# A two-branch encoder block on one core: where its small preparations stand, and which engine does them

## The chip, the core and the metric

The kernel runs on one core of a Trainium2 chip. The engines that matter are TensorE (PE in the profile; PEld is its weight load), VectorE (DVE), ScalarE (ACT), GpSimd (POOL) and SyncE (SP), whose queue issues the transfers. Each engine takes its instructions strictly in the order in which they stand in its own queue, and waits at semaphores for the others. The metric is the time of one execution in microseconds of the device. Four threads of the text run through all stages: the 128 x 512 matmul in fp32r as the unit of TensorE's work, the order of each queue, the PSUM banks, and the SP queue.

## The reference

One layer over a sequence of 1024 tokens of width 1024, all in float32. `x` is normalised and modulated, projected once, run through two token mixers in parallel, merged by gates, and followed by a SwiGLU feed-forward part. Cut to what matters here:

```python
u = layer_norm(x) * (1.0 + sc1) + sh1
proj = u @ w_in            # q, f, i, g | z, xbc, dt | gate_a, gate_b
# HGRN2, 8 heads of 128 x 128 states: f = lb + (1 - lb) * sigmoid(f_logit)
S_t = diag(f_t) S_{t-1} + (1 - f_t) i_t^T ;  o_t = S_t^T q_t
y_a = rms_norm(o, w_gnorm) * silu(g) @ w_branch_a
# Mamba-2, 4 groups of 8 heads: xbc = silu(causal_dwconv(xbc))
S_t = exp(a_t) S_{t-1} + b_t (delta_t x_t)^T ;  y_t = S_t^T c_t + d x_t
y_b = rms_norm(y * silu(z)) * w_norm @ w_branch_b
h = (sigmoid(gate_a) * y_a + sigmoid(gate_b) * y_b) @ w_o
x = layer_norm(ALPHA * x + g1 * h)
u = layer_norm(x) * (1.0 + sc2) + sh2
x = layer_norm(ALPHA * x + g2 * (silu(u @ w_gate) * (u @ w_up)) @ w_down)
```

## The kernel before

**Matmuls.** Full float32 accuracy comes from three fp32r matmuls for each contraction tile: low by high, high by low, high by high (`Dense.mm`, L81 to L83). The high part of an operand is a cast on ScalarE, the low part a subtraction on VectorE or GpSimd (`split`, L190 to L192; for weights `Dense.load`, L75 and L76). Such an operand is late when either is late. A *unit* is 128 output columns: two halves of 512 tokens, each of eight contraction tiles. The three matmuls of one contraction tile are called a subunit below.

**Stages.** In the profiled execution they lie as follows. 0 to 127: layer norm, modulation and the front of the input projection. 127 to 355: the other blocks, taken in pairs by a scheme that saves matmuls (`rest`). 355 to 500: the projection of `i` with the Mamba step sizes. 507 to 827: HGRN. 827 to 1300: Mamba. From 1300: the two branches' output matmuls (`dqs`), the merged projection, the first residual norm (to 1715) and the feed-forward part.

**Front.** The tokens come as 512 and 512 (`th` 0 and 1). The first four pairs run on half 0 while half 1 is normalised. Then comes a loop over `k` of four (from L413): `modulate(1, k)` and `modulate(1, 4 + k)`, a difference `c` of two tiles (L418) and four derived operands t1 to t4 with their splits; behind each step one further pair in `early`, which forms its weight difference (`combo`), splits it, multiplies, copies the product to `p1s` on ScalarE (L403) and subtracts it from a tile `ge` on VectorE (L405). The loop runs until seven pairs are done. Half 0 of gate block 6 follows.

**Projection of i.** Three groups of 352 columns over eight chunks of tokens. Behind group 0 the whole of `step_sizes` stands in the order: a chain of small VectorE operations to `adt`, a product with a triangular matrix (L527), and two transposing batches (L538), each in the same single PSUM bank "m", which `mod_segment` uses too.

**HGRN.** Eight heads of eight chunks of 128 tokens. `score(h, ch)` makes a chunk's scores, one chunk ahead: matmuls of 64, 32 and 16 columns on arrays `e` and `eb`, a copy `sc` on ScalarE (L687), two masked copies on VectorE (L689), a transposition and its copy `ks` (L693). `output` multiplies the scores (`oT`, L709) and updates the state with `ks`. In between `Fill` puts subunits of the next head's f and q projection and of gate units, about four a chunk (`share`). `prep(h)` makes a head's cumulated logarithms: five activations of 128 x 1024, eight scans (L620), two subtractions of 128 x 1024 (L627, L628). `arrays(h, hf)` makes the operands of half a head in six steps: four of `e` (L649, L654), one of `eb` (L657, L660), one of `kd` and `qd`. At chunk 3 the whole `prep(h + 1)` stands in the order, and the steps of `arrays` follow by twos at chunks 0 to 2 (second half) and 4 to 6 (next head).

**Mamba.** Four groups of eight chunks; `prepare` transposes x (`trx`, L850) one chunk ahead, `mix` has the inter-chunk (`yx`) and intra-chunk (`yi`) products; twelve subunits a chunk fill in, among them the next group's x, B and C blocks. The convolution's taps are VectorE operations on each half; `held` keeps two finished blocks for one Silu of 128 x 1024 each, the last x block too (L137). `squares` multiplies half a group by `z` on GpSimd (L923), squares and sums; `finish` has two matmuls `smm`, the norm's factors and four stores `yb_d` on SP. For the last group `squares(3, 0)` stands behind chunk 5, and everything else behind chunk 7, with 8 subunits ahead of the last `smm` and 24 behind it.

The order in each queue follows from a scheduler that takes the code's order as its base.

## Time and profile before

| | us |
|---|---|
| median of 3 runs | 2356.25 (2351.94 to 2360.98) |
| the profiled execution's own time | 2355.2 |
| its span, first to last instruction | 2353.3 |
| TensorE busy in it | 2251.6 (96%), mean granted clock 0.980 |
| VectorE, ScalarE, GpSimd busy | 1573.2, 1036.3, 314.7 |

A row of the timeline has the start, the length, engine, line, operation and tiles; in brackets the idle time of the engine before it and who ended it. Matmuls overlap: a wide one of 0.39 us starts about every 0.23 us. A row of windows has the stretch and its length, then busy time with the number of instructions in brackets for PE, PEld, DVE, ACT and POOL, then the granted clock of TensorE (1.00 is full speed), the DMA share and GB/s. A row of waits has the total in microseconds, the number of times and the longest. A row of groups has the number of instructions, busy time, mean in ns, and idle time before them. A line number is that of the kernel before.

### The profile page before, as it was taken

What the parts mean: (1) busy time and instruction counts of PE and PEld (TensorE: products, weight loads), DVE (VectorE), ACT (ScalarE), POOL (GpSimd) and SP (SyncE); (2) the same over time, 40 slices, a digit from 0 to 9 for tenths busy, and PEclk for the clock granted to TensorE, in tenths of its full rate; (3) what the DMA queues carried; (4) which work ended last, traced back from release to release, by engine and by line L of the source; (5) the groups of instructions that cost most, each with busy time, mean ns of one, the idle gap of its engine ahead of it and who ended that gap; (6) DMA issues with size and microseconds to landing.
All of it is one profiled execution on the core that took longest, in us unless ns stands there. A gap on an engine that the chain in (4) does not pass through costs nothing.

```text
span 2353.3 us, 32121 instructions
## 1 busy us (share of the span) xinstructions
PE 2251.6 (96%) x12412; PEld 1827.9 (78%) x12412; DVE 1573.2 (67%) x2545; ACT 1036.3 (44%) x1832; POOL 314.7 (13%) x188
## 2 busy tenths in 40 slices
PE   7889999999999999998997999999999999999998
PEld 4678888877777787777775788888778888888886
DVE  5966655538878657888976434458887666653556
ACT  3533333037666645777776411123533333322221
POOL 0600010011212121322223000003410000000000
PEclk9999999999999999999999999999999999999999
DMA  7344325611111232334355744423132222244553
GB/s 277 100 141 140 126 91 176 228 39 51 55 55 60 77 99 72 116 124 123 130 158 169 232 155 140 139 94 139 72 131 99 94 72 91 79 146 146 175 190 132
DMA packets 119504, 290.22 MB, mean 123 GB/s; under 512 B 12084, under 2 KB 26932, under 8 KB 119352
## 3 DMA queue, kind: packets, MB, share of 16 engines
q1 hardware_dynamic: 119352, 288.19, 36.6%
q8 instruction: 97, 1.59, 0.3%
q14 instruction: 55, 0.45, 0.1%
HBM read 234.52 MB, written 53.62 MB: 122 GB/s over the span
## 4 chain that ended last, share of the span: by engine, by line
PE 73%; DVE 10%; ACT 6%; DMA 3%; POOL 1%; issue 1%; SPq 0%; DVEq 0%; POOLq 0%; ACTq 0%
PE dps L81 9%; PE dps L82 9%; PE dps L83 9%; PE fps L81 9%; PE fps L82 9%; PE fps L83 8%; PE dqs L82 4%; PE dqs L83 4%; PE dqs L81 4%; DVE eb L657 1%; PE hps L83 1%; PE hps L82 1%; PE hps L81 1%; PE yi L897 1%; DVE e L649 1%
## 5 line engine op out<-in xcount | busy, mean ns | idle before, releaser
L81 PE MATMUL dps<-uh,wl 128*128 128x512 f32 x800 | 332.7, 416 | 2.5 <-DVE ge L405 2.5
L83 PE MATMUL dps<-uh,wh 128*128 128x512 f32 x800 | 318.6, 398 | 0.0
L82 PE MATMUL dps<-ul,wh 128*128 128x512 f32 x800 | 318.0, 398 | 0.0
L76 POOL TENSOR_TENSOR wl<-raw,wh 128x1024 fp32r<-128x1024 f32 x50 | 130.5, 2609 | 551.6 <-ACT wh L75 464.9
L81 PEld LDWEIGHTS dps<-uh,wl 128*128 128x128 f32 x800 | 156.0, 195 | 37.4 <-issue 9.9
L83 PEld LDWEIGHTS dps<-uh,wh 128*128 128x128 f32 x800 | 153.2, 191 | 33.9
L82 PEld LDWEIGHTS dps<-ul,wh 128*128 128x128 f32 x800 | 153.8, 192 | 28.5 <-issue 0.9
L179 POOL TENSOR_TENSOR mv<-mv,kc 128x1 f32<-128x1 f32 x32 | 32.8, 1032 | 1024.2 <-DVE mv L178 1016.2
L82 PE MATMUL dqs<-yp,wh 128*128 128x512 f32 x384 | 149.4, 390 | 0.0
L81 PE MATMUL dqs<-yp,wl 128*128 128x512 f32 x384 | 148.4, 389 | 0.9 <-ACT yp L191 0.9
L83 PE MATMUL dqs<-yp,wh 128*128 128x512 f32 x384 | 149.1, 389 | 0.0
L191 ACT CAST cw<-raw 128x512 fp32r<-128x512 f32 x131 | 80.7, 621 | 130.0 <-PE fps L83 86.7
L81 PE MATMUL fps<-t,cw 128*128 128x512 f32 x352 | 137.0, 389 | 0.7 <-ACT p L1177 0.7
L82 PE MATMUL fps<-t,cw 128*128 128x512 f32 x352 | 136.9, 389 | 0.0
L83 PE MATMUL fps<-t,cw 128*128 128x512 f32 x352 | 136.9, 389 | 0.0
L75 ACT CAST wh<-raw 128x1024 fp32r<-128x1024 f32 x75 | 78.4, 1046 | 112.3 <-PE dqs L83 103.5
L82 PE MATMUL fps<-wl,hp 128*128 128x512 f32 x304 | 118.4, 389 | 0.0
L83 PE MATMUL fps<-wh,hp 128*128 128x512 f32 x304 | 118.3, 389 | 0.0
L81 PE MATMUL fps<-wh,hp 128*128 128x512 f32 x304 | 117.0, 390 | 0.5 <-ACT wh L191 0.5
L192 DVE TENSOR_TENSOR wl<-wdr,wh 128x1024 fp32r<-128x1024 f32 x38 | 46.5, 1224 | 105.0 <-ACT wh L191 105.0
L192 DVE TENSOR_TENSOR cw<-raw,cw 128x512 fp32r<-128x512 f32 x109 | 79.9, 734 | 41.6 <-ACT cw L191 40.3
L191 ACT CAST wh<-wdr 128x1024 fp32r<-128x1024 f32 x38 | 40.1, 1054 | 147.3 <-PE fps L83 146.1
(367 smaller groups left out, 5649.2 us busy)
## 6 DMA issues: line engine op xcount, KB each, us to landing
raw<-in_w_blk_dram SPq DMA_DIRECT2D x78, 512.0 KB, 3.3
wdr<-in_w_d_dram SPq DMA_DIRECT2D x44, 512.0 KB, 3.9
wa<-in_w_ada_dram SPq DMA_DIRECT2D x32, 512.0 KB, 4.5
ac<-ac_d SPq DMA_DIRECT2D x32, 512.0 KB, 5.0
raw<-in_w_g_dram SPq DMA_DIRECT2D x26, 512.0 KB, 3.9
raw<-in_w_u_dram SPq DMA_DIRECT2D x26, 512.0 KB, 3.4
hr<-h_d SPq DMA_DIRECT2D x44, 256.0 KB, 4.0
h_d<-sg SPq DMA_DIRECT2D x18, 512.0 KB, 2.9
```

The lines of the kernel that those rows point to most:

```text
L75: nc.scalar.copy(wh, raw)
L76: (eng or self.lo).tensor_tensor(wl, raw, wh.bitcast(F32), op=ALU.subtract)
L81: nc.tensor.matmul(ps, sl, mh, start=first, stop=False)
L82: nc.tensor.matmul(ps, sh, ml, start=False, stop=False)
L83: nc.tensor.matmul(ps, sh, mh, start=False, stop=last)
L179: G.tensor_tensor(mv[:, 2:3], mv[:, 1:2], kc[:, 2:3], op=ALU.pow)
L191: S.copy(hi, src)
L192: eng.tensor_tensor(lo, src, hi.bitcast(F32), op=ALU.subtract)
L649: V.tensor_tensor(d.rearrange("p (n h j) -> p n h j", h=2, j=c), view(e, t0, (2 * c, n), (T + c, 2), (1, c)), view(r, t0 // 4 + c // 4 - 1 ...
L657: V.tensor_tensor(d.rearrange("p h (n j) -> p h n j", j=8), view(e, t0, (T, 2), (8, TH // 8), (1, 8)), view(r, t0 // 4, (T // 4, 2), (2, T ...
L897: PE.matmul(yi[64 * e:64 * e + 64, j, :], xd[:, HP * hh:HP * hh + HP], ac[:, hh, :], start=True, stop=True)
```

## The change

It has six parts; from the branch stage on each queue has the same instructions in the same order.

1. Front: `early` splits on VectorE instead of GpSimd, as do `c` and t3 in the k loop; the affine modulation of half 1 goes to ScalarE; the two loads for each modulation step are issued one step earlier; half 0 of gate block 6, and of gate block 7 (formerly in HGRN's last chunks), stand inside the k loop at k = 1 and 3, with their weights' low part on VectorE.
2. `step_sizes` stops before its matmuls and goes on behind chunk 4 of group 1; the bank "m" becomes three.
3. HGRN: `prep(h + 1)` in five pieces at chunks 0 to 4, `arrays(h + 1, 0)` by threes at chunks 5 and 6; `finish` one chunk later; `ks` copied by ScalarE.
4. Gate block 7's first half is gone from HGRN's filler: 8 subunits fewer.
5. Mamba: the last x block of a group gets its Silu by halves, the first as soon as its convolution is done; `bt` copied by ScalarE.
6. Last group: `squares(3, 0)` behind chunk 4, `finish(3, 0)` behind chunk 6, the multiplications by `z` of the last half on VectorE, and 18 instead of 8 subunits ahead of the last `smm` in the code.

```diff
-        ps = psum.tile([P, TH], F32, tag="m", name="mps", bufs=1)
+        ps = psum.tile([P, TH], F32, tag="m", name="mps", bufs=3)
...
+        def load_mod(j):
+            for h in range(2):
+                nc.sync.dma_start(out=was[:, (2 * j + h) % 4], in_=w_mod[j, :, 4 * h:4 * h + 4, :])
...
         def modulate(th, kt):
             u = xT[th][:, kt, :]
-            V.tensor_scalar(u, u, modc[:, 8 + kt:9 + kt], modc[:, kt:kt + 1], op0=ALU.mult, op1=ALU.add)
+            if th:
+                S.activation(u, u, AF.Identity, bias=modc[:, kt:kt + 1], scale=modc[:, 8 + kt:9 + kt])
+            else:
+                V.tensor_scalar(u, u, modc[:, 8 + kt:9 + kt], modc[:, kt:kt + 1], op0=ALU.mult, op1=ALU.add)
...
             if j + 2 < KT:
                 modulation(j + 2)
+            if j + 3 < KT:
+                load_mod(j + 3)
...
-        def early(q, a11, a12, eng=G):
+        def early(q, a11, a12, eng=V):
...
-            G.tensor_tensor(c, u1, u0, op=ALU.subtract)
-            split(t3[0][:, k, :], t3[1][:, k, :], c, G)
+            V.tensor_tensor(c, u1, u0, op=ALU.subtract)
+            split(t3[0][:, k, :], t3[1][:, k, :], c, V)
...
+            if k % 2:
+                n = 6 + k // 2
+                for _ in dn.unit(dn.load(w_blk[B_GA + n]), uh, ul, gate_evac(0, n), (0,)):
+                    pass
...
-        for _ in dn.unit(dn.load(w_blk[B_GA + 6], eng=G), uh, ul, gate_evac(0, 6), (0,)):
-            pass
...
         V.scalar_tensor_tensor(a, delta, -1.0, hr[:, None, 1, :].broadcast_to([P, TT, 32]), op0=ALU.mult, op1=ALU.mult)
-        ps = pp.tile([P, TH], F32, tag="m", name="dtps", bufs=1)
+        yield
+        ps = pp.tile([P, TH], F32, tag="m", name="dtps", bufs=3)
...
+                if g == 1 and tt == 4:
+                    steps.drain()
             if g == 0:
-                step_sizes(sp, pp)
+                steps = Fill(step_sizes(sp, pp))
+                steps.to(1)
...
                 act(ef, ef, AF.Exp, scale=-1.0)
+                yield
                 act(b, ef, AF.Ln, bias=lb[:, 3, h:h + 1], scale=lb[:, 1, h:h + 1])
+                yield
                 for c in range(TT):
                     V.tensor_tensor_scan(b3[:, c, :], ones, b3[:, c, :], 0.0, op0=ALU.mult, op1=ALU.add)
+                    if c == TT // 2 - 1:
+                        act(ef, ef, AF.Ln, bias=lb[:, 4, h:h + 1], scale=lb[:, 5, h:h + 1])
+                        yield
                 act(eq, eq, AF.Ln, bias=kc[:, 4:5], scale=QS)
-                act(ef, ef, AF.Ln, bias=lb[:, 4, h:h + 1], scale=lb[:, 5, h:h + 1])
...
+                V.scalar_tensor_tensor(ef, ef, -110.0, b, op0=ALU.max, op1=ALU.subtract)
+                yield
                 V.tensor_tensor(eq, b, eq, op=ALU.subtract)
-                V.scalar_tensor_tensor(ef, ef, -110.0, b, op0=ALU.max, op1=ALU.subtract)
...
-                    V.tensor_copy(ks, sp_[:, 3, :])
+                    S.copy(ks, sp_[:, 3, :])
...
-                if ch == 3 and h + 1 < HA:
-                    prep(h + 1)
-                    nxt = arrays(h + 1, 0)
-                if ch % 4 < 3 if ch < 4 else (ch < 7 and h + 1 < HA):
-                    next(nxt, None)
-                    next(nxt, None)
-                if ch % 4 == 0 and i:
-                    finish(*((h, 0) if ch else (h - 1, 1)))
+                    ahead = chain(prep(h + 1), arrays(h + 1, 0)) if h + 1 < HA else iter(())
+                for gen, n in ((nxt, "22200000"[ch]), (ahead, "11111330"[ch])):
+                    for _ in range(int(n)):
+                        next(gen, None)
+                if ch % 4 == 1 and i > 1:
+                    finish(*((h, 0) if ch > 4 else (h - 1, 1)))
...
-                        if th and len(held) == 2:
+                        if th and len(held) == 2 or held[-1][0] == 4 * g + 3:
                             for k, t in held:
+                                if k == 4 * g + 3:
+                                    t = t[:, TH * th:TH * th + TH]
                                 act(t, t, AF.Silu, bias=cl[:, C_CB + k:C_CB + k + 1])
-                            held.clear()
+                            held[:] = held[1:] if len(held) == 2 and not th else []
...
-                    V.tensor_copy(bt, cb[:, 1, :])
+                    S.copy(bt, cb[:, 1, :])
...
-                    G.tensor_tensor(xT[:, j, sl], xT[:, j, sl], zs, op=ALU.mult)
+                    (V if g == GB - 1 and hf else G).tensor_tensor(xT[:, j, sl], xT[:, j, sl], zs, op=ALU.mult)
...
-                if g == GB - 1 and ch == 5:
+                if g == GB - 1 and ch == 4:
                     squares(g, 0)
+                if g == GB - 1 and ch == 6:
+                    finish(g, 0)
                 fill.to(share(i + 1))
-            finish(g, 0)
             squares(g, 1)
-            fill.to(total + 8)
+            fill.to(total + 18)
             finish(g, 1)
```

In the queues this stands as follows; a row has the line, the operation, the tiles and their shape, and xN for N like it in a row. Line numbers of the changed kernel are its own, up to 22 higher.

GpSimd's queue before, through the k loop of the front (`cw` are weight differences of `early`, `ge` is `c`, `t_643` is t3):

```order
L192 TENSOR_TENSOR cw<-raw,cw 128x512 x2
L179 TENSOR_TENSOR mv<-mv,kc 128x1
L192 TENSOR_TENSOR cw<-raw,cw 128x512 x2
L418 TENSOR_TENSOR ge<-xT_106 128x512
L192 TENSOR_TENSOR t_643<-ge,t_643 128x512
L192 TENSOR_TENSOR cw<-raw,cw 128x512 x2
L418 TENSOR_TENSOR ge<-xT_106 128x512
L192 TENSOR_TENSOR t_643<-ge,t_643 128x512
L192 TENSOR_TENSOR cw<-raw,cw 128x512 x3
L418 TENSOR_TENSOR ge<-xT_106 128x512
```

And in the changed kernel, from the same place on, behind the scalar work of the norms:

```order
L179 TENSOR_TENSOR mv<-mv,kc 128x1 x8
L76 TENSOR_TENSOR wl<-raw,wh 128x1024 x6
L760 TENSOR_TENSOR y<-y,sq 128x512
L76 TENSOR_TENSOR wl<-raw,wh 128x1024
L760 TENSOR_TENSOR y<-y,sq 128x512
L76 TENSOR_TENSOR wl<-raw,wh 128x1024
```

All splits of the front have left this queue; the next rows are low parts of weights (L76) and the HGRN outputs' multiplications.

VectorE's queue before, around the preparation of an HGRN head (`b`, `r` and `ab` belong to `prep`; `e`, `eb` and `qd` to `arrays`; `sc` is the masked copy and `S` the state of the head that runs):

```order
L192 TENSOR_TENSOR csl<-sq,csh 128x512
L620 SCALAR_TENSOR_TENSOR b<-mk,b 128x128 x8
L717 SCALAR_TENSOR_TENSOR S<-S,ebl,st_ps 128x128
L625 COPY r<-b 128x256
L626 TENSOR_SCALAR r<-b 128x256
L627 TENSOR_TENSOR ab<-b,ab 128x1024
L628 SCALAR_TENSOR_TENSOR ab<-ab,b 128x1024
L689 COPY_PREDICATED sc<-mk,sc_ps_3616 128x128
L649 TENSOR_TENSOR e_5474<-ab,r 128x512
L689 COPY_PREDICATED sc<-mk,sc_ps_3616 128x128
L693 COPY ks<-sc_ps_3616 128x128
L649 TENSOR_TENSOR e_5478<-ab,r 128x512
```

And in the changed kernel:

```order
L638 SCALAR_TENSOR_TENSOR b<-mk,b 128x128 x8
L682 TENSOR_TENSOR eb<-eb,xq 128x512
L711 COPY_PREDICATED sc<-mk,sc_ps_3654 128x128 x2
L739 SCALAR_TENSOR_TENSOR S<-S,ebl,st_ps 128x128
L645 COPY r<-b 128x256
L690 TENSOR_TENSOR qd<-qd,xq 128x512
L646 TENSOR_SCALAR r<-b 128x256
L647 SCALAR_TENSOR_TENSOR ab<-ab,b 128x1024
L711 COPY_PREDICATED sc<-mk,sc_ps_3653 128x128 x2
L739 SCALAR_TENSOR_TENSOR S<-S,ebl,st_ps 128x128
L649 TENSOR_TENSOR ab<-b,ab 128x1024
L671 TENSOR_TENSOR e_5114<-ab,r 128x512
```

Between the scans and the last subtraction of the preparation there now stand two chunks' masked copies and state updates, where there was one state update.

VectorE's queue before, from the last chunk of Mamba to the branch (`yt` combines the two products, L942 is the norm's multiplication, L927 the sum of squares, `csl` the split of the sums):

```order
L901 TENSOR_TENSOR yt<-yx,eb 128x512
L910 TENSOR_TENSOR yt<-yt,yi 128x512
L913 TENSOR_TENSOR xTm<-xTm,yt 128x4x128
L942 SCALAR_TENSOR_TENSOR xTm<-xTm,cl,sqs 128x512 x4
L927 TENSOR_TENSOR sqs<-sqs,zs 128x512 x3
L192 TENSOR_TENSOR csl<-sqs,csh 128x512
L942 SCALAR_TENSOR_TENSOR xTm<-xTm,cl,sqs 128x512 x4
L76 TENSOR_TENSOR wl<-raw,wh 128x1024
```

And in the changed kernel:

```order
L922 TENSOR_TENSOR yt<-yx,eb 128x512
L963 SCALAR_TENSOR_TENSOR xTm<-xTm,cl,sqs 128x512 x4
L931 TENSOR_TENSOR yt<-yt,yi 128x512
L934 TENSOR_TENSOR xTm<-xTm,yt 128x4x128
L944 TENSOR_TENSOR xTm<-xTm,zs 128x512 x2
L948 TENSOR_TENSOR sqs<-sqs,zs 128x512
L944 TENSOR_TENSOR xTm<-xTm,zs 128x512
L948 TENSOR_TENSOR sqs<-sqs,zs 128x512
L944 TENSOR_TENSOR xTm<-xTm,zs 128x512
L948 TENSOR_TENSOR sqs<-sqs,zs 128x512
L192 TENSOR_TENSOR csl<-sqs,csh 128x512
L76 TENSOR_TENSOR wl<-raw,wh 128x1024
```

The first half's multiplication by its norm (x4) moved ahead of the last chunk's combination, the multiplications by `z` (L944) came in from GpSimd, and a weight's low part stands ahead of the last norm's multiplications.

More of the change, by code (lines that the diff above doesn't have):

```diff
@@ L229, in mod_segment @@
                 if nh:
-                    ps = psum.tile([P, TH], F32, tag="m", name="mps", bufs=1)
+                    ps = psum.tile([P, TH], F32, tag="m", name="mps", bufs=3)
                 PE.matmul(ps[0:1, :], ones[:, 0:1], acc[:, TH * nh:TH * nh + TH], start=True, stop=True)
@@ L252, in gate_evac, with gate_units @@
         return evac
-    def gate_units(which, n0, n1, fine=False):
+    def gate_units(which, n0, n1, fine=False, ths=(0, 1)):
         for n in range(n0, n1):
-            yield from dn.unit(w_blk[(B_GA, B_GB)[which] + n], uh, ul, gate_evac(which, n, fine), fine=fine)
+            yield from dn.unit(w_blk[(B_GA, B_GB)[which] + n], uh, ul, gate_evac(which, n, fine), ths, fine=fine)
     def combo(pool, tag, src, eng=V, **k):
@@ L342, in hybrid_block @@
         V.tensor_copy(cond32[:, :, 0], cond)
+        for j in range(2):
+            load_mod(j)
         for tt in range(4):
-            if tt < 2 and MF > tt:
+            if tt < 2:
                 modulation(tt)
@@ L362, in hybrid_block @@
         for n in range(2):
-            if MF <= n:
-                modulation(n)
+            if n:
+                load_mod(2)
             for q in (2 * n, 2 * n + 1):
@@ L535, in step_sizes @@
         for hf in range(2):
-            ps = pp.tile([P, TH], F32, tag="m", name="dtps", bufs=1)
+            ps = pp.tile([P, TH], F32, tag="m", name="dtps", bufs=3)
             for j in range(4):
@@ L741, in hgrn_phase @@
             units = [dense_fq(h) for h in range(HA)]
-            fill = Fill(chain(*units, gate_units(0, 7, 8, True), gate_units(1, 0, NGB, True)))
+            fill = Fill(chain(*units, gate_units(0, 7, 8, True, (1,)), gate_units(1, 0, NGB, True)))
             fill.to(HF0)
-            prep(0)
-            for _ in arrays(0, 0):
-                pass
+            for g in (prep(0), arrays(0, 0)):
+                for _ in g:
+                    pass
             fill.to(HF1)
             score(0, 0)
-            total = 16 * (2 * HA + 1 + NGB)
+            total = 16 * (2 * HA + NGB) + 8
             def share(i):
@@ L756, in share @@
                 return a + (total - a) * (i - 8 * HA + 12) / 12
-            nxt = None
             for i in range(8 * HA):
```

5 lines of the change are left out of this document (3 added, 2 removed).

## The prediction

> **What bounds the kernel now.** I read the page's busy table first, then the waits of TensorE (PE), then windows of single stages.
>
> ```profile
> PE 2251.6 (96%) x12412; PEld 1827.9 (78%) x12412; DVE 1573.2 (67%) x2545; ACT 1036.3 (44%) x1832; POOL 314.7 (13%) x188
> 177.00:236.00 59.00, 59.00 (x262) 48.83 (x262) 40.68 (x64) 22.02 (x35) 0.00 (x0) 1.00 0.42 141
> 59.00:118.00 59.00, 48.84 (x195) 37.60 (x194) 53.79 (x65) 33.05 (x58) 40.53 (x25) 0.91 0.31 102
> ```
>
> TensorE is busy 96% of the span and sets the end. In a stretch without loss (second row) it issues 262 wide matmuls in 59.00 us, 0.225 us each. I call three of them, one contraction tile, a subunit: 0.68 us. Since the change leaves the number of matmuls as it is, it can gain only where TensorE waits, or runs at a lower granted clock behind a wait. In the front (last row) it issued 195, at a granted clock of 0.91 (the last but two of the columns), so (262 - 195) x 0.225 = 15 us were lost there. The waits name the other places:
>
> ```profile
> PE trx L850 <- ACT xTm L137: 13.5, 3, 6.7
> PE smm L936 <- DVE csl L192: 12.5, 1, 12.5
> PE dps L81 <- DVE cw L192: 10.2, 5, 4.9
> PE sc_ps L683 <- DVE eb L660: 7.6, 6, 1.4
> PE dps L81 <- DVE ge L405: 6.6, 3, 3.9
> PE dtps L527 <- DVE adt L524: 2.9, 1, 2.9
> ```
>
> The columns are microseconds in total, number of waits, longest. Each lies in a stage that the diff touches, except part of the third. They sum to 53 us.
>
> **Front: forecast -6 us.** The change takes all `early` splits and the t3 work from GpSimd to VectorE.
>
> ```profile
> L192 POOL TENSOR_TENSOR cw<-raw,cw 128x512 fp32r<-128x512 f32 x14 | 22.1, 1584 | 9.3 <-ACT cw L191 9.3
> L418 POOL TENSOR_TENSOR ge<-xT 128x512 f32<-128x512 f32 x4 | 9.0, 2251 | 2.9 <-DVE xT L318 2.9
> L192 POOL TENSOR_TENSOR t<-ge,t 128x512 fp32r<-128x512 f32 x4 | 6.0, 1504 | 3.7 <-ACT t L191 3.7
> 82.04 0.68 DVE L421 TENSOR_TENSOR xT<-xT,ul 128x512 f32<-128x512 f32 x1
> 82.64 0.67 DVE L405 TENSOR_TENSOR ge<-p1s,dps 128x512 f32<-128x512 f32 x1
> ...
> 88.40 1.77 DVE L421 TENSOR_TENSOR xT<-xT,ul 128x512 f32<-128x512 f32 x1
> ```
>
> The first three rows are GpSimd's groups in 59 to 118: 22 operations that VectorE now has to do. Then the same VectorE instruction without and with a GpSimd split running: 0.68 and 1.77 us; alone, the next one starts 0.60 behind it. So VectorE's 53.79 us of 59 hold 65 operations that alone would take 65 x 0.60 to 0.68, 39 to 44 us. After the change it has 22 more, and 4 to 8 fewer (the second half's modulate goes to ScalarE; eight in all, not all of them in this stretch): 79 to 83 operations, 47 to 56 us. TensorE's own work there is 195 x 0.225 = 44, and the gate half-unit moved in adds 24 x 0.225 = 5.4, with a split of a 128x1024 weight on VectorE (two such operations, 1.2 to 1.4), a cast, a load and a sigmoid. So the stretch, the half-unit inside, takes 49 on TensorE and 48 to 57 on VectorE, where it took 59: between -11 and -2. Waits of one for the other in order add to the larger of the two. I take -6, bounds -1 and -12. The modulation loads leave SP one step earlier; what they stand ahead of there are weight loads that are issued many steps before their use, so I cost them at nothing.
>
> The activation tables change four more times here. The row of a load (below, at 1200.26) is 1.28, and ScalarE was busy 33.05 of 59, so 5.1 us more hide in its idle time. Were that cover gone, all 5.1 would be added. The Trainium skill, "ScalarE: Activation LUTs", What ACT_TABLE_LOAD costs, adds a drain of about 1380 ns to each switch; the row behind the load below starts 1.29 after it, so the trace does not show it. By the page, and with nothing hidden, the sum would be 10.6 us higher.
>
> **Step sizes: -4 us.** The generator stops before its matmuls until chunk 4 of the next column group, and its tiles get three banks instead of one.
>
> ```profile
> 411.60 0.70 PE L527 MATMUL dtps<-adt,mk 128*128 128x256 f32 x2 [2.95 <-DVE adt L524]
> 415.24 1.63 PE L538 MATMUL dtps<-mk,adt 128*32 128x128 f32 x8
> ```
>
> The wait of 2.95 goes, since VectorE finishes `adt` long before chunk 4, and the lower clock behind a wait with it. With one bank, besides, the second batch of L538 must wait for the first's copy, which it need no longer. I put these two at 1 us together. Bounds -2 and -6.
>
> **HGRN heads: -22 us.** Each head costs the same 32 subunits before and after.
>
> ```profile
> 646.66 0.39 PE L709 MATMUL oT<-sc,i_sb 128*128 128x128 f32 x2
> ...
> 650.99 0.39 PE L709 MATMUL oT<-sc,i_sb 128*128 128x128 f32 x2
> ...
> 643.00:659.70 16.70, 16.70 (x194) 13.11 (x193) 10.20 (x26) 12.68 (x23) 3.85 (x2) 1.00 0.08 30
> 673.50:681.00 7.50, 6.12 (x63) 4.73 (x62) 7.47 (x11) 5.43 (x13) 2.04 (x1) 1.00 0.22 78
> 643.00:681.00 38.00, 36.43 (x392) 28.15 (x391) 31.48 (x68) 25.85 (x49) 8.22 (x4) 1.00 0.16 56
> 672.07 4.56 DVE L657 TENSOR_TENSOR eb<-ab,r 128x1024 f32<-128x1024 f32 x2
> 677.28 0.27 PE L683 MATMUL sc_ps<-eb 128*32 128x32 f32 x8 [1.38 <-DVE eb L660]
> L693 DVE COPY ks<-sc_ps 128x128 f32<-128x128 f32 x7 | 2.0, 283 | 0.0
> ```
>
> A chunk with four subunits takes 4.33 us (first two rows), so eight take 34.6, against 38.0 for a head: 3.4 lost, 27 over eight heads. The windows say where. In the first half of a head TensorE never rests and VectorE works 10.20 of 16.70; then a preparation arrives whole, and VectorE works 7.47 of 7.50 while TensorE waits for `eb`. The change spreads the preparation over chunks 0 to 4 and the arrays over 5 and 6, and gives the seven `ks` copies (2.0 us) to ScalarE. VectorE's demand falls to 29.5 of 34.6 us (85%), ScalarE's rises to 25.85 + 7 x 0.28 = 27.8 (80%): both fit, though engines that work in order at 85% still make TensorE wait at times. I leave 1.3 us a head, so 27 becomes 10: -17, and the gate half-unit that moved to the front is 5.4 us less here: -22. The bounds: the moved work and a little, -8; all stalls but 0.7 us a head, -27. `finish` moves one chunk later; its output is first read by the branch, which starts at 1315 (below).
>
> **Mamba edges: -5 us.**
>
> ```profile
> 1189.80 0.49 PE L850 MATMUL trx<-mk,xTm 128*128 128x128 f32 x3
> ...
> 1200.29 0.47 PE L850 MATMUL trx<-mk,xTm 128*128 128x128 f32 x1 [4.32 <-ACT xTm L137]
> ...
> 1191.56 0.63 ACT L925 ACTIVATE zs<-xTm 128x512 f32<-128x512 f32 x1 [2.34 <-POOL xTm L923]
> ...
> 1199.10 1.15 ACT L137 ACTIVATE xTm<-xTm,cl 128x1024 f32<-128x1024 f32 x1
> 1200.26 1.28 ACT L135 ACT_TABLE_LOAD   x1
> 1201.55 1.06 ACT L137 ACTIVATE ac<-ac 128x1024 f32<-128x1024 f32 x1
> ...
> 1190.12 0.74 DVE L813 SCALAR_TENSOR_TENSOR xTm<-dps,cl,xTm 128x509 f32<-128x509 f32 x1
> ```
>
> The first chunk of the next group needs only the first half of the last x block, but the Silu takes both, so the fourth transposition waits until 1200.25. The first half's convolution ends at 1190.86; a Silu of that half could end near 1192.8, behind the square at 1191.56. But the order now puts all four transpositions first, at 1189.80, so TensorE would meet a wait of some 3 us there in place of the 4.32. Over three edges the 13.5 becomes about 9 to 10, and the halved clock behind each costs as before: -5, bounds 0 and -12. The `bt` copies go the way of `ks` and are hidden by six subunits.
>
> **End of Mamba: -9 us.**
>
> ```profile
> 1272.69 1.54 PE L897 MATMUL yi<-ac,xd 128*64 128x128 f32 x16 [2.25 <-ACT csh L191]
> 1296.07 0.80 PE L936 MATMUL smm<-csl,ones_r 128*128 128x512 f32 x1 [12.49 <-DVE csl L192]
> 1284.27 2.50 SPq L943 DMA_DIRECT2D yb_d<-xTm  x4
> 1287.65 0.56 SPq L922 DMA_DIRECT2D zs<-z_d  x1
> 1291.99 1.26 POOL L923 TENSOR_TENSOR xTm<-xTm,zs 128x512 f32<-128x512 f32 x1 [8.29 <-DMA zs<-z_d]
> 1301.97 0.90 SPq L1008 DMA_DIRECT2D yr<-ya_d  x2
> L191 ACT CAST yp<-yr x8: 1033/1046/1052, 1307.1 to 1329.2; 128x1024 fp32r<-128x1024 f32 x8
> L81 PE MATMUL dqs<-yp,wl x21: 388/389/499, 1315.0 to 1329.4; 128*128 128x512 f32 x21
> ```
>
> From the last intra-chunk product (ends 1274.2) to the branch's first matmul (1315.0) are 40.8 us, with 3 + 8 + 24 = 35 subunits in TensorE's queue, 23.9 us. So 17 are lost: 12.49 waiting, the rest at the lower clock. The wait is for the fourth gating load `zs`, which stands on SP behind four stores of the first half, which wait for that half's norm. The change ends the first half in chunk 6, multiplies on VectorE (0.68 against 1.26) and puts 21 subunits (14.3 us) ahead of the sums. Without the 8.29 the chain of 21.9 us from 1274.2 to 1296.07 shrinks to about 13.5: hidden. But 14 subunits (9.5 us) remain behind the sums. There the old rows show what is late next: the loads `yr` leave SP only after the second half's stores, the first operand cast ends 12 us behind the sums (1308.1 - 1296.1), its VectorE split follows, and all eight take 22 more. I put a new wait there at 4 to 9 us, so of 17 I keep 9; bounds -2 and -14.
>
> **Sum.** -6 - 4 - 22 - 5 - 9 = -46 against the profiled execution's 2355.2 us: 2309. The median of the runs shown is 1 us above it, so 2310. From the branch stage on no instruction changes its order.
>
> **Rivals.** (1) HGRN stays bound by VectorE: it keeps 85% of the time, in order, and scans or `ab` operations between two chunks delay the masks just as `eb` did. Then the stage gains only the bound of 8, 14 less: 2324. For it: `sc_ps` already waits for `eb` in six places; against: the 16.70 of 16.70 beside a VectorE at 61%. (2) The branch's operands bind: the end of Mamba gains 2, not 9: 2317. For it speaks the row of 22 us; against, that 24 subunits hid nearly all of it and the stores now start earlier. (3) Slower: the `ks` copy stands on ScalarE behind long activations of the same preparation, and the state product needs it in each of 56 chunks. A 128x1024 activation takes 1.15 (the row at 1199.10). If every chunk lost that, 64 us would go: 2310 + 64 = 2374. It turns the forecast's sign above 46 / 56 = 0.82 us a chunk. Against it: the product stands two subunits (1.4 us) behind the scores, and a preparation has five such activations for eight chunks. (4) The table rule above, unhidden: 2310 + 10.6 = 2321.
>
> **How the numbers follow.** Forecast 0.60, rival 1 0.18, rival 2 0.11, rival 3 0.05, rival 4 0.01, the remaining 0.05 for several losses at once (about 2340). The likeliest case's own range: 2295 to 2322. For 8 in 10 the range runs from nearly all good bounds (2356 - 71 = 2285, taken as 2288) to rival 1 with the weak end of Mamba and little in the front (2356 - 22 = 2334). A measurement of this kernel tells 0.5%, 12 us, from no change. Rivals 1, 2 and 4 are still faster than that; rival 3 is no change between 0.6 and 1.0 us a chunk and slower above. Faster 0.90, same 0.06, slower 0.04.
>
> **What would show it.** After the change GpSimd has no 128x512 operation before 130 us, and VectorE's all take 0.7 or less there. The `dtps` wait is gone. `oT` starts every 4.3 us in all heads; a head of 37 or more with VectorE full proves rival 1. The `smm` wait is under 2 us, and a wait of `dqs` for `yp` names rival 2. A wait of `st_ps` for ScalarE's `ks` names rival 3. I am wrong if the time is above 2334, or if the stages from the branch on change their length by over 3 us.

## The result

The changed kernel takes 2317.6 us (median of four runs, 2310.2 to 2321.1) against 2355.0 for the kernel before beside it (four runs, 2351.9 to 2361.0): a ratio of 0.9834, interval 0.9803 to 0.9865. Run again on another occasion with more rounds it took 2318.9 against 2355.2, ratio 0.9845 (0.983 to 0.986). So it is faster by 1.6%, some 37 us. The forecast was 2310, 46 us less, with a range of 2288 to 2334.

The profiled execution of the changed kernel was the quickest of its four, 2310.2 us with a span of 2308.4, and 7 us below the median. One trace is therefore not enough to share 37 us out among stages. Twelve further traces of experiments (below) leave most stages as the changed kernel has them, and the mean over all traces whose code in a stage is that of the changed kernel is steadier. From the first matmul on, in microseconds:

| stage, from the order of TensorE | before | changed: mean (lowest to highest), traces | difference | forecast |
|---|---|---|---|---|
| front and pairs, to the i projection | 354.9 | 351.0 (349.8 to 351.6), 12 | -3.9 | -6 |
| i projection | 112.3 | 106.2 (103.2 to 107.6), 8 | -6.1 | -4 |
| HGRN, to its last `oT` | 345.6 | 324.1 (321.1 to 325.4), 11 | -21.5 | -22 |
| Mamba, first `trx` to group 3's first `yi` | 312.5 | 307.8 (305.8 to 312.4), 12 | -4.7 | -5 |
| group 3's first `yi` to the branch's last matmul | 365.3 | 366.0 (363.6 to 367.9), 9 | +0.7 | -9 |

They sum to -35.5, near the 37 of the medians. The column before has one trace.

### The profile page after: what moved, and what is told of

Same layout as the page of the kernel before. It is cut to its first block, busy times and chain, and to the rows that moved or that the text cites. A ratio compares the mean times of both kernels' runs of the same rounds, so it can differ in the third digit from the quotient of the medians.

```text
span 2308.4 us, 32125 instructions
## 1 busy us (share of the span) xinstructions
PE 2230.2 (97%) x12412; PEld 1816.2 (79%) x12412; DVE 1567.8 (68%) x2489; ACT 1061.6 (46%) x1931; POOL 264.8 (11%) x153
## 4 chain that ended last, share of the span: by engine, by line
PE 82%; DVE 8%; ACT 3%; issue 3%; DMA 2%; POOL 2%; SPq 0%; DVEq 0%; POOLq 0%; ACTq 0%
PE dps L81 11%; PE dps L83 11%; PE dps L82 11%; PE fps L81 9%; PE fps L82 9%; PE fps L83 9%; PE dqs L81 4%; PE dqs L83 4%; PE dqs L82 4%; PE hps L83 1%; PE hps L81 1%; PE hps L82 1%; PE sc_ps L701 1%; DVE xTm L832 1%; PE yi L918 1%
## 5 line engine op out<-in xcount | busy, mean ns | idle before, releaser
L81 PE MATMUL dps<-uh,wl 128*128 128x512 f32 x800 | 331.7, 415 | 3.3 <-POOL wl L76 3.3
L76 POOL TENSOR_TENSOR wl<-raw,wh 128x1024 fp32r<-128x1024 f32 x49 | 132.1, 2696 | 790.4 <-ACT wh L75 723.4
L81 PEld LDWEIGHTS dps<-uh,wl 128*128 128x128 f32 x800 | 155.1, 194 | 37.6 <-issue 6.6
L81 PE MATMUL dqs<-yp,wl 128*128 128x512 f32 x384 | 147.5, 393 | 6.6 <-ACT yp L191 4.3
L83 PE MATMUL dqs<-yp,wh 128*128 128x512 f32 x384 | 150.1, 391 | 0.0
L81 PE MATMUL fps<-t,cw 128*128 128x512 f32 x352 | 137.0, 389 | 0.7 <-DVE cw L192 0.7
L192 DVE TENSOR_TENSOR cw<-raw,cw 128x512 fp32r<-128x512 f32 x131 | 94.8, 725 | 43.5 <-ACT cw L191 42.2
L81 PE MATMUL fps<-wh,hp 128*128 128x512 f32 x304 | 117.0, 390 | 0.5 <-ACT wh L191 0.5
```

The source lines that it names most:

```text
L76: (eng or self.lo).tensor_tensor(wl, raw, wh.bitcast(F32), op=ALU.subtract)
L81: nc.tensor.matmul(ps, sl, mh, start=first, stop=False)
L83: nc.tensor.matmul(ps, sh, mh, start=False, stop=last)
L192: eng.tensor_tensor(lo, src, hi.bitcast(F32), op=ALU.subtract)
```

## The profile after

The busy line of the page and the longest waits of TensorE in the changed kernel (total, number of times, longest):

```profile
PE 2230.2 (97%) x12412; PEld 1816.2 (79%) x12412; DVE 1567.8 (68%) x2489; ACT 1061.6 (46%) x1931; POOL 264.8 (11%) x153
```

```profile
PE dps L81 <- DVE cw L192: 15.4, 9, 4.5
...
PE trx L871 <- ACT xTm L137: 7.4, 2, 4.0
PE dqs L81 <- ACT yp L191: 4.3, 1, 4.3
...
PE yi L918 <- ACT csh L191: 3.2, 1, 3.2
PE yx L910 <- DVE Sm L927: 3.0, 2, 2.5
...
PE dtps L539 <- issue: 2.1, 1, 2.1
```

The line of 12.5 us, `smm` for `csl`, is gone, and so are the six waits for `eb` and the three for `ge` in the front. The total for weight differences (`cw`) on VectorE is longer (10.2 before), but the 5.3 us that TensorE waited for GpSimd's are gone, so together they are the same. Three waits at the end of Mamba have grown: `yi` from 2.3 to 3.2, `yx` from 1.3 to 3.0, and `dqs` for the branch's first operand from 0.9 to 4.3.

The windows of the changed kernel, the front's stretch and one whole head of HGRN (columns as before; PE, PEld, DVE, ACT, POOL, then the granted clock):

```profile
59.00:118.00 59.00, 51.72 (x220) 41.53 (x219) 50.05 (x87) 48.92 (x76) 1.10 (x2) 0.91 0.38 128
627.40:644.50 17.10, 17.10 (x196) 13.50 (x195) 16.18 (x32) 12.64 (x28) 4.42 (x2) 1.00 0.17 57
627.40:662.50 35.10, 35.10 (x394) 27.69 (x393) 31.24 (x61) 27.23 (x58) 9.15 (x4) 1.00 0.18 62
```

TensorE does not rest in the head at all: 35.10 of 35.10, beside a VectorE that is busy for 31.24 of it (89%). In the front it issues 220 matmuls in the 59 us where it issued 195, with VectorE doing 87 operations instead of 65 in less time.

## The experiments

Each starts from the changed kernel; line numbers are those of the kernel that is run. Where a stage is compared, the table's spread of the unchanged stage is the yardstick.

### HGRN with the whole preparation at chunk 3

```diff
-                for gen, n in ((nxt, "22200000"[ch]), (ahead, "11111330"[ch])):
+                for gen, n in ((nxt, "22200000"[ch]), (ahead, "00072220"[ch])):
```

> The changed kernel, with the preparation of the next HGRN head whole at chunk 3 again and its arrays by twos at chunks 4 to 6; the ks copies stay on ScalarE. Theory (staging gives the gain): heads go from 35.1 us back to 37 or more, because VectorE is full for some 15 us in a row and the scores wait for eb; the stage from the end of the i projection to the last oT goes from 322 to about 340, the whole from 2317 to 2335. Rival (taking seven copies a head off VectorE is what gave it): heads stay below 36, the whole within 4 us of the changed kernel.

Measured: 2341.4 us, ratio 0.9939 (0.992 to 0.9958). The stage takes 348.9 us, against 321.1 to 325.4. From the second head on, heads take 37.9 to 39.7 us. Its windows and its longest wait in the stage:

```profile
651.00:659.50 8.50, 6.41 (x59) 4.77 (x58) 8.50 (x16) 3.47 (x8) 3.94 (x1) 1.00 0.06 18
...
637.60:677.00 39.40, 37.31 (x393) 28.91 (x392) 30.88 (x62) 27.26 (x57) 9.02 (x5) 0.96 0.16 55
```

```profile
PE oT L731 <- DVE sc L711: 10.9, 6, 2.1
```

The theory holds in kind: the head in this kernel has the same VectorE work as the staged one (30.88 against 31.24), only its place differs, and the stage is 24.8 us longer than the mean. In the stretch in which the preparation arrives VectorE is busy 8.50 of 8.50 and TensorE 6.41. But the edit is more crowded than the expectation says, and more than the kernel before. The preparation has five steps, so a 7 at chunk 3 puts two steps of `arrays` there as well, and the other four follow at chunks 4 and 5. The order of before would have given about 340 us here (345.6 less the 5.4 of the gate half-unit that moved away), so the 24.8 us are not the size of what the change gained, and how they divide between the preparation and those two steps is not shown. VectorE's masked copies `sc` around the preparation, in this kernel and then in the changed one:

```profile
645.70 0.64 DVE L711 COPY_PREDICATED sc<-mk,sc_ps 128x128 f32<-128x128 uint32 x2 [2.15 <-ACT sc L709]
...
655.74 0.31 DVE L711 COPY_PREDICATED sc<-mk,sc_ps 128x128 f32<-128x128 uint32 x1
655.93 3.29 DVE L671 TENSOR_TENSOR e<-ab,r 128x512 f32<-128x512 f32 x2
659.14 0.29 DVE L711 COPY_PREDICATED sc<-mk,sc_ps 128x128 f32<-128x128 uint32 x1
```

```profile
626.75 0.30 DVE L711 COPY_PREDICATED sc<-mk,sc_ps 128x128 f32<-128x128 uint32 x1
...
632.94 0.63 DVE L711 COPY_PREDICATED sc<-mk,sc_ps 128x128 f32<-128x128 uint32 x2
```

What is late is not `eb` but `sc`. Between the copies of two chunks stand 9.40 us of other work, against 5.89 in the changed kernel, and the chunk's second copy stands behind two operations on `e`.

### The ks copies back on VectorE

```diff
-                    S.copy(ks, sp_[:, 3, :])
+                    V.tensor_copy(ks, sp_[:, 3, :])
```

> The changed kernel, with only the ks copies back on VectorE. Theory: VectorE goes from 85 to 91% in a head, and heads from 35.1 to 35.5 or so, +0 to +6 us on the whole. Rival 3 of the prediction (ScalarE is late with ks): heads get shorter by 0.3 us or more, waits of the state product for ks vanish. If VectorE were the bound (rival 1), +16 us (56 copies x 0.28).

Measured: 2318.0 us, ratio 0.9844 (0.9821 to 0.9868), the same as the changed kernel. The stage takes 321.6 us. One head:

```profile
627.40:662.50 35.10, 35.10 (x393) 27.70 (x392) 32.39 (x69) 26.12 (x49) 8.88 (x4) 1.00 0.18 62
631.60:650.30 18.70, 18.70 (x204) 14.80 (x202) 18.63 (x40) 12.94 (x25) 4.33 (x2) 1.00 0.17 58
```

VectorE is now busy for 32.39 of 35.10, 92%, and still TensorE does not wait. The second row is the stretch in which the preparation arrives: VectorE works 18.63 of 18.70 us there, so a full VectorE is not by itself what makes the scores late. So the copies cost nothing on either engine: rival 1 (VectorE binds) and rival 3 (ScalarE is late with `ks`) both fall, and this part of the change could have been left out.

### One bank in the i projection, and the step sizes in one piece

```diff
-        ps = psum.tile([P, TH], F32, tag="m", name="mps", bufs=3)
+        ps = psum.tile([P, TH], F32, tag="m", name="mps", bufs=1)
...
-        ps = pp.tile([P, TH], F32, tag="m", name="dtps", bufs=3)
+        ps = pp.tile([P, TH], F32, tag="m", name="dtps", bufs=1)
```

> The changed kernel, with one bank m instead of three in the i projection; step_sizes still in two parts. The stage fell from 112.3 to 103.3 us. Theory: the banks give about 1 us, the rest is where the step sizes stand: the stage stays within 103 to 105. Rival: the banks free the modulation's column product from waiting, and without them its 5.7 us of loss return: about 109.

Measured: 2320.2 us, ratio 0.985 (0.9824 to 0.9875). The stage takes 107.6 us, at the upper edge of the 103.2 to 107.6 that the unchanged code shows, so the banks alone can't be told from nothing. And the other half:

```diff
                 steps = Fill(step_sizes(sp, pp))
-                steps.to(1)
+                steps.drain()
```

> The changed kernel, with step_sizes whole behind group 0 again and three banks. Theory: the wait of dtps for adt is 3 us again and the VectorE work of the modulation is late again behind the step sizes' chain: 110 to 112 us for the stage. Rival (banks): 104 to 106, as only the adt wait returns.

Measured: 2319.5 us, ratio 0.9848 (0.9822 to 0.9875). The stage takes 110.3 us, 4 more than the mean and outside its spread; in the whole time that is not told from nothing. TensorE in this kernel, and then in the changed one, with VectorE's rows of the changed one around it:

```profile
409.62 1.22 PE L539 MATMUL dtps<-adt,mk 128*128 128x256 f32 x2 [5.07 <-DVE adt L535]
```

```profile
416.72 0.67 PE L539 MATMUL dtps<-adt,mk 128*128 128x256 f32 x2 [2.09 <-issue]
```

```profile
408.21 1.28 DVE L217 SCALAR_TENSOR_TENSOR acc<-wa,cond,acc 128x1024 f32<-128x1024 f32 x1 [0.32 <-DMA wa<-in_w_ada_dram]
...
410.88 3.41 DVE L217 SCALAR_TENSOR_TENSOR acc<-wa,cond,acc 128x1024 f32<-128x1024 f32 x1
...
416.20 0.42 DVE L535 SCALAR_TENSOR_TENSOR adt<-delta,hr 128x256 f32<-128x256 f32 x1
```

The wait for `adt` did not go with the change. The page calls it "issue", but `adt` ends at 416.62 and the matmul starts at 416.72: it is the same wait. With the matmuls put off, the scheduler's order lets the modulation's sums (`acc`, which wait for their weights `wa`) in between the steps of the chain on VectorE, so `adt` comes just as late. In the eight traces with this code the wait goes from 1.7 to 4.5 us, and the stage from 103.2 to 107.6 with it. What differs is where GpSimd's work falls. These are `adt` and GpSimd's row beside it in the kernel before, then `adt` in the changed kernel when it was run again:

```profile
409.10 2.45 DVE L524 SCALAR_TENSOR_TENSOR adt<-delta,hr 128x256 f32<-128x256 f32 x1
408.65 5.11 POOL L76 TENSOR_TENSOR wl<-raw,wh 128x1024 fp32r<-128x1024 f32 x2 [70.91 <-PE dps L83]
```

```profile
414.78 2.52 DVE L535 SCALAR_TENSOR_TENSOR adt<-delta,hr 128x256 f32<-128x256 f32 x1
```

The same operation took 0.42 us in the row at 416.20 above, where GpSimd's low part of a weight (`wl`) started at 416.27, just behind it; in the two rows here such a `wl` was already running (the second from 414.69 to 417.03). In the two traces with 103.2 and 103.3 us neither `adt` nor the step ahead of it meets a `wl`; in the other six one of the two does and takes 2.4 to 2.6 us. In the kernel with the step sizes whole both do (2.58 and 2.60), and its wait is 5.07.

What did go is the modulation's own wait, `mps` for `acc`, at 439 in the kernel before:

```profile
PE mps L222 <- DVE acc L217: 2.3, 1, 2.3
```

With the lower clock behind it, TensorE's intervals from 436 to 448 are 5.8 us longer in sum than its steady ones. The changed kernel has no such wait. The kernels with one half of the edit have none at this line either, so which half removes it is not told apart. With the banks alone the stage takes 110.3, with the parts alone 107.6, with both 106.2 by the mean, against 112.3 before; whether the banks add anything to the parts is within the spread.

### The second part of the step sizes later

```diff
-                if g == 1 and tt == 4:
+                if g == 1 and tt == 6:
                     steps.drain()
```

> The changed kernel, with the second part of step_sizes behind chunk 6 of group 1 instead of chunk 4, some 9 us later. Theory: what is left of the dtps wait (1.7 to 4.0 us, adt stands among the modulation's sums on VectorE, and these wait for their weights) goes: the i projection takes 101 to 104 us, the whole 2 to 4 us less. Rival (the modulation's sums take any place that is free, so adt comes later as well): the wait stays over 1.5 us.

Measured: 2313.4 us, ratio 0.9821 (0.9807 to 0.9835); the changed kernel on the same chip 2318.9, 0.9845 (0.983 to 0.986). The stage takes 101.6 us. VectorE and TensorE:

```profile
416.77 0.42 DVE L535 SCALAR_TENSOR_TENSOR adt<-delta,hr 128x256 f32<-128x256 f32 x1
```

```profile
423.89 0.59 PE L539 MATMUL dtps<-adt,mk 128*128 128x256 f32 x2
```

`adt` is ready 6.7 us ahead and the wait is gone. In the two kernels below, which have this edit too, the stage takes 100.8 and 100.7 us. That settles the remaining wait: it was `adt`, and chunk 4 was too early for it, also where `adt` itself is quick (103.2 us).

### The front's splits back on GpSimd

```diff
-        def early(q, a11, a12, eng=V):
+        def early(q, a11, a12, eng=G):
...
-            V.tensor_tensor(c, u1, u0, op=ALU.subtract)
-            split(t3[0][:, k, :], t3[1][:, k, :], c, V)
+            G.tensor_tensor(c, u1, u0, op=ALU.subtract)
+            split(t3[0][:, k, :], t3[1][:, k, :], c, G)
```

> The changed kernel, with the splits of the early pairs, c and t3 back on GpSimd; the modulation of half 1 stays on ScalarE, the gate half-units stay in the loop. Theory: VectorE's 128x512 operations take 1.7 us again where a GpSimd split runs, and products wait for GpSimd's low parts: the i projection starts 6 to 12 us later than at 361.6, the whole is 2323 to 2329. Rival (VectorE is full in the changed front, so work taken from it helps): the i projection starts 1 to 4 us earlier.

Measured: 2333.3 us, ratio 0.9899 (0.9875 to 0.9922). The front takes 359.3 us, 8.3 more than the mean; the i projection then starts at 369.3. The stretch from 59, two groups of VectorE in it, and TensorE's wait for GpSimd:

```profile
59.00:118.00 59.00, 45.06 (x183) 34.57 (x182) 45.81 (x61) 42.77 (x68) 29.80 (x22) 0.91 0.32 103
```

```profile
L192 DVE TENSOR_TENSOR t<-xT,t 128x512 fp32r<-128x512 f32 x11 | 10.6, 981 | 0.3 <-ACT t L191 0.3
...
L430 DVE TENSOR_TENSOR xT<-xT,uh 128x512 f32<-128x512 f32 x4 | 5.3, 1338 | 3.6 <-POOL ge L428 3.6
```

```profile
PE dps L81 <- POOL cw L192: 11.3, 6, 4.4
```

The same two groups in the changed kernel:

```profile
L192 DVE TENSOR_TENSOR t<-xT,t 128x512 fp32r<-128x512 f32 x12 | 8.1, 688 | 0.8 <-ACT t L191 0.8
...
L430 DVE TENSOR_TENSOR xT<-xT,uh 128x512 f32<-128x512 f32 x4 | 2.7, 685 | 0.0
```

VectorE's operations take 0.98 and 1.34 us by the mean beside GpSimd's and 0.69 without: the theory holds, for 8 us in the stage. The rival falls; taking 22 operations from VectorE did not shorten the front. The whole time rose by 14 to 16 us, more than the stage. The profiled execution was the quickest of its four, 5.6 us below their median, and has only small parts more in the stages behind (HGRN 325.0, the end 367.6, at the upper edges of their spreads); where the rest lies, and what ties it to this edit, is not shown. The other parts of the front's change (the modulation on ScalarE, the earlier loads, the gate half-units inside the loop) were not tested by themselves.

### The last block's Silu whole

```diff
-                        if th and len(held) == 2 or held[-1][0] == 4 * g + 3:
+                        if th and len(held) == 2:
```

> The changed kernel, with the last x block's Silu whole again. Theory: the waits of the transpositions return; the three group lengths go from 96.6, 101.9, 98.9 back towards 99.9, 103.8, 100.5, +7 us in all, the whole 2324. Rival (the order of the queues and the bt copies gave it): groups stay within 1 us.

Measured: 2331.2 us, ratio 0.9894 (0.9869 to 0.9919). From the first `trx` to group 3's first `yi` it takes 315.0 us, 7.2 more than the mean and 2.6 more than the longest of the twelve. The transpositions' wait in this kernel:

```profile
PE trx L869 <- ACT xTm L137: 16.6, 3, 6.3
```

Against 7.4 us in the changed kernel: the theory holds for the stage. The time moved by 12 to 14; the other 5 to 6 are not assigned.

### The end of Mamba as before

```diff
-                if g == GB - 1 and ch == 4:
+                if g == GB - 1 and ch == 5:
                     squares(g, 0)
-                if g == GB - 1 and ch == 6:
-                    finish(g, 0)
...
+            finish(g, 0)
             squares(g, 1)
-            fill.to(total + 18)
+            fill.to(total + 8)
...
-                    (V if g == GB - 1 and hf else G).tensor_tensor(xT[:, j, sl], xT[:, j, sl], zs, op=ALU.mult)
+                    G.tensor_tensor(xT[:, j, sl], xT[:, j, sl], zs, op=ALU.mult)
```

> The changed kernel, with the end of Mamba as before: squares of the last group behind chunk 5, first half's finish after the loop, multiplications by z on GpSimd, 8 subunits. From the first yi of the last group to the last branch matmul the trace has about 1 us less after the change, though the 12.5 us wait is gone. Theory (the moves only carried the wait into the last chunks and to the branch's operands): the whole within 3 us of the changed kernel, the 12.5 us wait back. Rival (prediction): +9, 2326.

Measured: 2330.6 us, ratio 0.9889 (0.9861 to 0.9917), 12 more than the changed kernel. TensorE's waits in this kernel from 1200 to 1300, and from 1546 to 1701:

```profile
PE smm L957 <- DVE csl L192: 14.3, 1, 14.3
PE yx L910 <- DVE Sm L927: 2.6, 1, 2.6
PE dqs L81 <- ACT yp L191: 2.3, 2, 1.3
```

```profile
PE fps L81 <- DVE tm L1202: 5.8, 1, 5.8
PE dps L81 <- DVE tm L1202: 4.3, 1, 4.3
```

By the stage, the theory: the wait of 14.3 us is back, and yet from group 3's first `yi` to the branch's last matmul it takes 368.2 us against a mean of 366.0. By the whole time, the rival. The two go together only because this kernel's trace loses 6 us in the merged projection (154.9 against 148.5 to 150.1 in all others, two waits for `tm`) and 2.7 in the feed-forward part, behind the point from which the orders are equal. In the changed kernel `tm` is waited for once there, 2.9 us. VectorE's operations there run at 0.68 or 1.78 us as GpSimd's happen to lie beside them, so a shift can cost some microseconds; that this edit brings the shift about in every run is not shown, and where its 12 us come from stays half open: about 2 from group 3's first `yi` to the branch's last matmul, about 9 behind it. The 2 are a difference of two larger ones: up to the branch's first matmul this kernel takes 103.9 us against a mean of 98.3, in the branch's matmuls 264.3 against 267.7.

### Only the places as before

```diff
-                if g == GB - 1 and ch == 4:
+                if g == GB - 1 and ch == 5:
                     squares(g, 0)
-                if g == GB - 1 and ch == 6:
-                    finish(g, 0)
...
+            finish(g, 0)
             squares(g, 1)
```

> The changed kernel, with only the places of squares(3, 0) and finish(3, 0) as before; VectorE multiplies and 18 subunits stay. Theory: the waits in the last chunks (yx for Sm 2.5 and 0.6, yi for csh 3.2) shrink by 3 to 5 us, but the zs load stands behind the stores again and the sums wait 5 to 9 us: +2 to +5 on the whole. Rival (the stores do not hold the load up, VectorE's multiplications alone were enough): -3 to -5, the sums wait under 2.

Measured: 2312.9 us, ratio 0.9818 (0.9798 to 0.9837). From group 3's first `yi` to the branch's last matmul it takes 361.4 us, below all nine traces of the changed code (363.6 to 367.9), and the sums wait 0.6 us. So the rival was right and my theory wrong: the stores do stand ahead of the last `zs` load again, but with the longer cover in front of the sums nothing waits for it. Multiplying on VectorE and covering the chain together were the useful part (neither was tested without the other); moving the first half's norm into the last chunks was harmful.

### Both edits, and a later finish

> The changed kernel once more, on the chip of the next three and with more rounds. The four runs shown lie between 2310 and 2321; the profiled one was the fastest of them. Expected: median 2314 to 2320, and a trace in which the i projection takes 103 to 108 us, as in the seven kernels whose code there is the same.

Measured: 2318.9 us, as given above; the i projection 106.9 us.

> steps_later and tail_place together: the first half of the last group is finished after the loop again. Theory: the two gains add, -3 and -4 us: 2308 to 2312 against the changed kernel on the same chip at 2317. Rival (tail_place's 2313 was within the spread): the same as steps_later.

Measured: 2309.4 us (2307.9 to 2310.9), ratio 0.9801 (0.9787 to 0.9815). Beside the changed kernel's 0.9845 (0.983 to 0.986) on the same chip the two intervals are apart: 9.5 us less than the changed kernel and 45.8 less than the one before. The two gains about add. The stages: i projection 100.8 us, the end 360.3. TensorE at the end, first of this kernel, then of the changed one:

```profile
1223.99 1.16 PE L910 MATMUL yx<-cT,Sm 128*128 128x128 f32 x8 [2.51 <-DVE Sm L927]
1234.52 1.09 PE L918 MATMUL yi<-ac,xd 128*64 128x128 f32 x16 [0.69 <-ACT csh L191]
...
1254.73 0.49 PE L957 MATMUL smm<-csl,ones_r 128*128 128x512 f32 x1 [0.47 <-DVE csl L192]
...
1266.61 1.22 PE L81 MATMUL dqs<-yp,wl 128*128 128x512 f32 x2 [5.26 <-ACT yp L191]
```

```profile
1221.23 1.62 PE L910 MATMUL yx<-cT,Sm 128*128 128x128 f32 x8 [2.46 <-DVE Sm L927]
...
1227.36 1.16 PE L910 MATMUL yx<-cT,Sm 128*128 128x128 f32 x8 [0.57 <-DVE Sm L927]
1231.69 1.22 PE L918 MATMUL yi<-ac,xd 128*64 128x128 f32 x10 [3.17 <-ACT csh L191]
...
1253.18 0.39 PE L957 MATMUL smm<-csl,ones_r 128*128 128x512 f32 x1
...
1267.64 2.07 PE L81 MATMUL dqs<-yp,wl 128*128 128x512 f32 x4 [4.27 <-ACT yp L191]
```

With the first half's sums and norm taken out of the last chunks, the intra-chunk product waits 0.69 instead of 3.17 us. The wait of 5.26 for the branch's first operand stays. The waits are only part of the gain. From group 3's first `yi` to the branch's first matmul TensorE starts 485 matmuls in every kernel: in 102.7 us before, in 96.7 to 100.2 in the nine traces of the changed code, in 93.7 to 95.9 in the three with the places as before. It waits 10.1 to 12.3 us there in the nine and 8.9 to 10.8 in the three, and the granted clock is 0.94 to 0.96 against 0.97 to 0.98.

```diff
-                        if ch == f + 2:
+                        if ch == f + 2 + (g == GB - 1 and hf):
                             finish(g - 1, hf)
```

> As place_and_steps, and the second finish of group 2 stands one chunk later, behind chunk 6 of group 3. Theory: VectorE no longer sits idle 3.2 us before the four norm multiplications ahead of the state update, so the 2.5 us wait of yx for Sm goes: 2 to 4 us less than place_and_steps. Rival: the multiplications meet the sums of the first half instead, and the wait moves to csh and the last chunk: no gain or +2.

Measured: 2310.2 us, ratio 0.9804 (0.9786 to 0.9822), the same. The wait of `yx` for `Sm` is 3.6 us, not gone, and the sums wait 3.3 in two places. The rival holds: VectorE's norm multiplications meet the next thing instead.

## Why the prediction was right, and where it was not

**HGRN, -22: right, and right in kind.** The stage fell by 21.5 us. That the preparation in one place makes the scores late, and the same work in pieces does not, is what the first experiment shows, by its direction: with two steps of the arrays added to the pile it costs 24.8 us, so it does not give the size. Three details were off. I read the stretch in which VectorE worked 7.47 of 7.50 as the cause; but with the `ks` copies back VectorE worked 18.63 of 18.70 and TensorE went on, because the masked copies came in between. What counts is how long the operation that TensorE needs stands behind others. I wrote that 85% of an engine in order would still make TensorE wait at times, and left 1.3 us a head: at 89 and 92% TensorE did not wait in a head of 35.1 us. And I counted the `ks` copies as part of what makes room: they make no difference. That `finish` stands one chunk later was not tested by itself.

**Front, -6: right in kind, measured -3.9.** Work of 5.4 us came in on top, so the stalls fell by about 9. The term rested on the price of a VectorE operation beside GpSimd's, and the splits put back show it. What I did not see is what is late next. This window and these rows are of the changed kernel:

```profile
59.00:91.50 32.50, 25.22 (x103) 19.79 (x102) 26.64 (x51) 29.24 (x47) 1.10 (x2) 0.84 0.34 114
```

```profile
83.68 0.79 PE L81 MATMUL dps<-uh,cw 128*128 128x512 f32 x1 [4.49 <-DVE cw L192]
...
128.61 0.50 PE L81 MATMUL dps<-t,cw 128*128 128x512 f32 x1 [4.15 <-DVE cw L192]
```

ScalarE is busy 90% there, with the modulation added, and VectorE 82%; a weight difference stands in their queues behind the derived operands, and TensorE waits 4.49 us. From there on nothing waits until the first pair of the rest, at 128.61, whose weight differences come 4.15 us late.

**The tables: row against rule.** The prediction set the rule of the Trainium skill ("ScalarE: Activation LUTs", What ACT_TABLE_LOAD costs), a drain of about 1380 ns with each switch, beside a row that showed none. The changed kernel's trace does not agree with that rule either. Between 60 and 130 us it has six loads; behind five of them the next instruction starts 1.29 us after the load's start, which is the load, and behind the sixth it waits for TensorE. So rival 4 falls. One of the five:

```profile
109.61 1.28 ACT L135 ACT_TABLE_LOAD   x1
110.90 1.14 ACT L191 CAST t<-xT 128x512 fp32r<-128x512 f32 x2
```

**i projection, -4: the size near by luck, the step wrong.** The stage fell by 6.1, a little past the bound of -6, but the step "The wait of 2.95 goes, since VectorE finishes `adt` long before chunk 4" failed: a wait of 1.7 to 4.5 us stayed. I took a fixed chain on VectorE and moved only its reader; the order let other work into the chain as soon as its reader was put off. I also overlooked that about 2 of the 2.95 us came from GpSimd, beside which `adt` took 2.45 us instead of 0.42, though the price of such a meeting is what my term for the front rests on. The gain came from the modulation's wait of 2.3 us and its clock, which I had read in the list of waits and given no term.

**Mamba edges, -5: right.** -4.7, with the waits of the transpositions from 13.5 to 7.4 us in the profiled execution, and the single case counted as I said: a wait of some 3 to 4 us remains where all four transpositions stand first. Two small things came in that I had not counted: 1.5 us for `bt`, whose copies I had called hidden, and two waits for `wl` of GpSimd, 3.3 us in this trace and up to 6.3 in the others, where the kernel before has none. Why the second came is not shown.

**End of Mamba, -9: wrong.** It gave +0.7, outside its bounds of -2 to -14. The step that failed is "of 17 I keep 9": the list of what is late next was too short. It had the branch's operands (4 to 9 us), which came about as put: the start of the branch gained 4.3 us by the mean, and its matmuls lost 5.1. What it lacked is the last group itself. Moving `squares(3, 0)` and `finish(3, 0)` into chunks 4 to 6 puts their sums and multiplications on VectorE's queue ahead of the state and the products of those chunks. VectorE in the changed kernel shows the kind of step, for the norm of the group before:

```profile
1217.84 2.74 DVE L963 SCALAR_TENSOR_TENSOR xTm<-xTm,cl,sqs 128x512 f32<-128x512 f32 x4 [2.87 <-ACT sqs L137]
1220.49 0.68 DVE L927 TENSOR_TENSOR Sm<-Sm,sps 128x512 f32<-128x512 f32 x1
```

VectorE stands idle 2.87 us for a norm's factors that nobody needs soon, then multiplies for 2.7, and only then updates the state that TensorE waits for. I had costed this move by what it frees (SP's queue, the fourth `zs`) and not by the queues that it is put into. Without the move the end takes 360.3 to 362.4 us instead of 363.6 to 367.9, 3 to 5 less than before the change; of what is still missing to -9 the branch's matmuls, with their late operands, account for 3.4 to 3.9.

**From the branch on: a sign that I had named.** I had written that the instructions keep their order from the branch on, and that a change of over 3 us in a stage there would prove me wrong. The branch's matmuls took 265.7 to 270.0 us in the nine traces, against 262.7 before. In the trace their order is not the same at the start either: four of L81 stand first in a row (the row at 1267.64), where the lines alternated before. Behind the branch the changed kernel is within 2 us of the one before in each of its nine traces.

**Rivals.** Rival 1 and rival 3 fell by their own experiments. Rival 2, the branch's operands, is what happened, though with a second cause beside it: it said 2317, and that is where the kernel is. I gave it 0.11. That the forecast of 2310 is still only 8 us off is in part luck: the end missed by 10, and 2 of these came back in the i projection by a way that I had not foreseen.

## What to carry to other kernels

An engine at 90% of a stage need not hold anything up, and one at 80% may, and a stretch without a gap need not either: look for the operation that the bounding engine waits for, and at how much other work stands ahead of it in its queue, and cut that work up before moving some to another engine. When a block of work is moved to an earlier place, list what it now stands in front of in every queue it enters, above all operations that will wait there for something late; a wait removed at the end can come back in small pieces ahead of it. When the reader of a chain is put off, the chain is put off too, unless something else holds it in place: leave the reader more room than the chain's old length. Before a single trace's difference is called a gain, see how far the stage moves between traces of the same code.

## What the runs showed of the hardware that was not expected

VectorE's operation on `adt`, 128 x 256, took 0.42 us alone and 2.4 to 2.6 us when GpSimd's 128 x 1024 `wl` (2.3 to 2.6 us) had started before it or with it; begun just ahead of such a `wl` it took 0.42. In eight traces of the same code the i projection took 103.2 and 103.3 us where neither `adt` nor the step ahead of it met a `wl`, and 106.6 to 107.6 where one of them did.

Code that is the same also took 321.1 to 325.4 us in HGRN and 305.8 to 312.4 in Mamba's first three groups, from one execution or kernel to the next, at a whole time that varied by 11 us over the first four runs of the changed kernel; the causes of these are not shown. From the first gate unit to the i projection it was far steadier, 270.0 to 270.1 us in twelve traces. One trace against one trace can mislead by 4 to 6 us for a stage of the first kind.
